# A two-layer mixture-of-experts trunk: routing taken off GpSimd, three experts in fixed places, the sorted lists made later, and the last weight tiles in the right pool

## The chip, the cores and the metric

The kernel runs on one core of a Trainium2 chip. The metric is the device time of one execution in microseconds (us). The core's engines are TensorE (PE in the profile; PEld is its weight load), VectorE (DVE), ScalarE (ACT), GpSimd (POOL) and SyncE (SP), which issues most of the transfers; SPq in a view is SyncE's queue.

## The reference, cut to what matters

1,024 tokens of 1,024 values go through two layers. A layer is a mixer (layer 0: gated DeltaNet and a diagonal state space; layer 1: dilated attention), an output projection with residual and layer norm, and a mixture of experts (MoE), again with residual and layer norm:

```python
x <- LayerNorm(alpha * x + sublayer(x)), alpha = (2*DEPTH)**0.25
D_MODEL = 1024; SEQ = 1024; EXPERT_FF = 512
MOE_GROUPS = 4; EXPERTS_PER_GROUP = 8; N_EXPERTS = 32; MOE_TOP_K = 2
```

Each token picks the best of four groups by its logits, then two of the group's eight experts; the sum of the two experts' outputs, silu(x Wg) * (x Wu) times Wd each, is weighted by gates made from the logits. How many tokens an expert gets is known only in the run.

## The kernel before, in words

**Stages.** By time of the trace: mixer of layer 0 and its output stage to about 650 us, MoE of layer 0 to 1201, its combine, the value projection and attention to 1880, the output stage of layer 1, its MoE from 1915 to 2458, the last combine to the end. The Tile framework orders the instructions of each engine by a timeline of its own; `issue_after(x)` lets an instruction be placed only after x.

**Output stage and routing.** `out_stage` works through eight token tiles of 128 rows. `logits` (`lgP`, `lgd`, `lg`) gives the router's logits, `route` picks experts and counts each token's place in its expert (`rM`, `rrk`, `rcnt`), `layer_norm` writes the normed rows to `hd` in memory (`hd<-or`). Of tile 7, the last, the norm's scale runs on ScalarE and its product with g and sum with b on GpSimd (L223, L226). At the end of `route` stand the token lists: `first` (lists of the large places; its first FIXED = 2 are experts 0 and 1 as they are), made at L354 and L355. `sort` (`osort`, `soP`, `soQ`) then ranks the 32 experts by their counts and writes `order`, `first` of places 2 to 15 and `small`; `gates` the gates and each token's `place`; `overflow` (`ofP`, `over`) plans blocks for experts with too many tokens. All three stand in the output stage.

**MoE.** 32 experts, six weight loads of 1 MB each (`wraw<-in_wm`, L458). Places 0 to 15 are large (128 tokens, `large`): each half tile of weights is split into a high part on ScalarE (`whi`, L486) and the remainder on VectorE (`wlo`, L489), and TensorE multiplies hi and lo parts of rows and weights three times (L528, L529, L546). Twelve halves a large expert. Places 16 to 31 are small (64 tokens, `small`), multiplied straight from the loaded tiles (L583, L599). The sequence is 0, 1, then per j the smalls s_j and s_(j+8) and two larges. A gather (L495, GpSimd) fetches an expert's rows of `hd` by its list; TensorE transposes them (`px`, L503), ScalarE and VectorE split them (`xh`, `xl`); one gather serves two smalls. Outputs are scattered to `yd` by GpSimd. After the fourth expert `table` writes sixteen index columns (`tab`, L428), read only in the overflow loop. Loads go in a ring of 17 tiles, ten in the left pool (`RAW`) and seven in the right (`RAWB`); two, later three, are in flight; the first ten are issued during the output stage. The halves have a ring of six. `moe_rest` holds the overflow loop, which runs zero times here, behind a barrier of all engines.

**Behind the MoE.** In layer 0 the value projection's four weight loads (`wraw<-in_wv`, L916) go into tiles of the left pool, in the ring's size, and two tiles of `hd` (`ca`) are loaded ahead. In layer 1 all eight are, in a pool that begins behind the place of the ring's last tiles, and `fg`, `fb` (norm weights, L191) after them. `combine` loads `yd` (`cy`), and in layer 1 TensorE sums gate-weighted rows (`cp`, L758); in four tiles (`SUMMED` = 1, 3, 5, 7) ALPHA * rows too, in the other four VectorE adds it (L762).

Of the kernel before, what the change touches and what calls it, by code (L numbers as in the profile page):

```python
# [32 lines left out]
FIXED = 2  # L33
# [120 lines left out]
class Trunk:  # L154

    SUMMED = (1, 3, 5, 7)

# [201 lines left out]
    def sort(self, R, first, small, order, ps):  # L359
# [3 lines left out]
        w = R["sort"]  # L363
        key, hot, tmp, tab = w[:NE, 0:32], w[:NE, 32:64], w[:NE, 64:96], w[:NE, 128:256]
        kp, rank = w[:NE, 96:97], w[:NE, 97:98]
        ident = self.ident[:NE, :NE]
        nc.vector.scalar_tensor_tensor(key, R["cnt"][:NE], float(NE), self.c("keyb")[:NE], op0=OP.mult, op1=OP.add)
# [6 lines left out]
        nc.tensor.transpose(p[:NE, :128], R["tab"], self.ident)  # L374
# [8 lines left out]
        nc.vector.tensor_copy(R["rank"], p[:, 96:128])  # L383
# [83 lines left out]
    def weights(self, src):  # L467
# [11 lines left out]
        for c in range(2):  # L479
# [126 lines left out]
    def moe(self, l, hd, yd, first, small, order, place, xp, wk, ps):  # L606
# [32 lines left out]
        next(run)  # L639
        next(run)  # L640
        for i in range(NE):
# [12 lines left out]
            if i == 3:  # L654
                with tc.issue_after(st.ins):
                    self.table(l, place)

# [24 lines left out]
    def overflow(self, R, over, ps):  # L682
# [3 lines left out]
        w = R["sort"][:BLOCKS]  # L686
        cap, c, cum, one, le, f = (w[:, i * NE:(i + 1) * NE] for i in range(6))
        ci = R["over"][:BLOCKS]

        idx = self.c("pidx")[:BLOCKS]  # L690
        nc.vector.tensor_scalar(cap, R["rank"][:BLOCKS], float(LARGE) - 0.5, None, op0=OP.is_lt)
        nc.vector.scalar_tensor_tensor(c, cap, -64.0, R["cnt"][:BLOCKS], op0=OP.mult, op1=OP.add)
# [24 lines left out]
    def ahead(self, l, hd, p, ts):  # L717
# [1376 lines left out]
```

## Time and profile before

| what | value |
|---|---|
| runs | 2517.41, 2521.05, 2521.86 us, median 2521.05 |
| the profiled execution's own time | 2522.76 us |
| its span | 2520.9 us |
| TensorE busy | 2276.8 us, 90% |
| VectorE busy | 1466.6 us, 58% |
| ScalarE busy | 1146.6 us, 45% |
| GpSimd busy | 485.0 us, 19% |
| MoE of layer 0, first transposes to the last matmul | 657.58 to 1201.1 us |
| MoE of layer 1, end of its last matmul | 2458.35 us |

Busy shares are averages over stages with different limits. A view of stretches tells, for each piece of the span, the busy time of each engine, the clock granted to TensorE (PEclk, a share of 2.4 GHz) and the mean busy share of the DMA engines. A row of waits names the waiting engine and line, whom it waited for, the total, how often and the longest. A row of a timeline begins with start and duration.

### The profile page before, as it was taken

How to read it: one execution, taken by the hardware profiler on the slowest of the kernel's cores; microseconds unless marked ns; L12 is line 12 of the kernel's file. 1: busy time of each engine (PE TensorE's matmuls, PEld its weight loads, DVE VectorE, ACT ScalarE, POOL GpSimd, SP SyncE). 2: the span in 40 equal slices, each digit the busy share in tenths (PEclk: the TensorE clock that was granted, in tenths of full speed). 3: DMA queues.
4: the chain of work that ended last, by engine and by line, in shares of the span. 5: the costliest groups of instructions: out<-in, count | busy, mean ns of one | idle time of the engine just before them, and what ended most of it. 6: DMA issues, size and time to landing. Idle time of an engine off the chain costs nothing. (4 is left out here: it accounts for less than half of the span.)

```text
span 2520.9 us, 33905 instructions
## 1 busy us (share of the span) xinstructions
PE 2276.8 (90%) x11950; PEld 1629.8 (65%) x11950; DVE 1466.6 (58%) x2901; ACT 1146.6 (45%) x1871; POOL 485.0 (19%) x566
## 2 busy tenths in 40 slices
PE   7999999899697999998599999997996979999986
PEld 5888888678454555555477777775784545555552
DVE  7655656556853555554554766766468535555545
ACT  5436353442453444443324666666325534444432
POOL 1445433102231111110001111103113311111100
PEclk9999999899798999999799999998997989999997
DMA  4222222272599999999531000102725999999986
GB/s 162 61 64 50 57 79 68 102 272 86 220 365 401 411 404 402 400 399 390 178 124 34 30 31 26 41 24 83 270 74 206 375 398 410 405 405 407 401 334 252
DMA packets 179198, 560.82 MB, mean 222 GB/s; under 512 B 59200, under 2 KB 96448, under 8 KB 129360
## 3 DMA queue, kind: packets, MB, share of 16 engines
q1 hardware_dynamic: 163920, 525.01, 55.1%
q0 software_dynamic: 15104, 33.60, 3.6%
q8 instruction: 96, 1.57, 0.2%
q14 instruction: 78, 0.64, 0.1%
HBM read 518.76 MB, written 55.36 MB: 228 GB/s over the span
## 5 line engine op out<-in xcount | busy, mean ns | idle before, releaser
L489 DVE TENSOR_TENSOR wlo<-wraw,whi 128x1024 fp32r<-128x1024 f32 x380 | 447.8, 1220 | 139.9 <-ACT whi L486 136.9
L486 ACT ACTIVATE whi<-wraw 128x1024 fp32r<-128x1024 f32 x384 | 384.4, 1053 | 76.2 <-PE pu L529 36.2
L583 PE MATMUL pgs<-wraw,xs 128*64 128x512 f32 x1024 | 241.3, 603 | 0.0
L583 PEld LDWEIGHTS pgs<-wraw,xs 128*64 128x64 f32 x1024 | 70.1, 138 | 133.4 <-issue 129.9
L172 PE MATMUL pj<-xTh,phi 128*128 128x512 f32 x320 | 131.9, 417 | 13.6 <-ACT xTh L449 13.6
L1072 POOL TENSOR_TENSOR plo<-praw,phi 128x256 fp32r<-128x256 f32 x64 | 50.2, 786 | 437.6 <-ACT phi L1071 291.4
L172 PE MATMUL pj<-xTh,plo 128*128 128x512 f32 x320 | 132.5, 415 | 0.0
L172 PE MATMUL pj<-xTl,phi 128*128 128x512 f32 x320 | 131.1, 410 | 0.0
L971 DVE CUSTOM_DVE_ANT_0 sm<-s,amask 128x1024 f32<-128x1024 f32 (+7 forms) x128 | 96.6, 756 | 51.5 <-PE s L967 49.6
L528 PE MATMUL pg<-whi,xh 128*128 128x512 f32 x256 | 107.0, 418 | 18.9 <-ACT whi L486 13.8
L599 PE MATMUL pos<-wraw,hs 128*64 128x512 f32 x512 | 118.6, 598 | 5.7 <-ACT xh L449 3.3
L988 PE MATMUL pp<-cf,sm 128*128 128x128 f32 x576 | 100.8, 285 | 22.8 <-ACT pt L992 18.0
L172 PE MATMUL opo<-ohi,oyp 128*128 128x512 f32 x392 | 115.7, 403 | 2.4 <-DVE oyp L450 2.4
L1088 PE MATMUL pj<-xTh,phi 128*128 128x512 f32 x256 | 114.6, 448 | 2.9 <-ACT phi L1071 1.0
L528 PE MATMUL pg<-wlo,xh 128*128 128x512 f32 x256 | 108.2, 423 | 8.1 <-DVE wlo L489 7.8
L551 POOL DMA_INDIRECT yd<-ot,first x32 | 38.0, 1188 | 369.2 <-issue 178.8
L975 ACT ACTIVATE sm<-sm,st 128x1024 f32<-128x1024 f32 (+7 forms) x128 | 99.1, 775 | 18.7 <-DVE st L974 16.4
L988 PEld LDWEIGHTS pp<-cf,sm 128*128 128x128 f32 x576 | 68.4, 143 | 57.8 <-ACT pt L992 50.0
L528 PE MATMUL pg<-whi,xl 128*128 128x512 f32 x256 | 103.4, 404 | 0.0
L529 PE MATMUL pu<-wlo,xh 128*128 128x512 f32 x256 | 102.4, 400 | 0.0
L529 PE MATMUL pu<-whi,xl 128*128 128x512 f32 x256 | 102.3, 400 | 0.0
L529 PE MATMUL pu<-whi,xh 128*128 128x512 f32 x256 | 102.2, 399 | 0.0
(543 smaller groups left out, 5195.7 us busy)
## 6 DMA issues: line engine op xcount, KB each, us to landing
wraw<-in_wm SPq DMA_DIRECT2D x384, 1024.0 KB, 8.3
cy<-yd SPq DMA_DIRECT2D x32, 512.0 KB, 7.3
praw<-in_win SPq DMA_DIRECT2D x40, 256.0 KB, 2.7
oraw<-in_wo SPq DMA_DIRECT2D x16, 512.0 KB, 3.3
hd<-or SPq DMA_DIRECT2D x16, 512.0 KB, 3.2
ca<-hd SPq DMA_DIRECT2D x16, 512.0 KB, 5.9
praw<-in_wqk SPq DMA_DIRECT2D x64, 128.0 KB, 2.3
oy<-ytd SPq DMA_DIRECT2D x14, 448.0 KB, 4.5
```

The costliest lines, as they stand in the source:

```text
L172: self.last = self.nc.tensor.matmul(*args, **kw).ins
L486: nc.scalar.activation(hi, r[:, h], AF.Copy)
L489: eng.tensor_tensor(lo, r[:, h], hi.bitcast(F32), op=OP.subtract)
L528: nc.tensor.matmul(pg, x[:, k], w[:, 0:512], start=s, stop=z)
L529: nc.tensor.matmul(pu, x[:, k], w[:, 512:1024], start=s, stop=z)
L583: nc.tensor.matmul(pg[r].rearrange("p (g f) -> p g f", g=2), x[:, k], w[:, k % 2, a], start=(k == 0), stop=(k == KT - 1))
L599: nc.tensor.matmul(po[r], hs[:, f % 2, f // 2], W[f // 2][:, o:o + 512], start=(f == 0), stop=(f == 3))
L971: nc.vector.tensor_tensor_reduce(out=sm[:, :n], in0=s[:, :n], in1=am[:, 1024 - n:1024], scale=1.0, scalar=-3e38, op0=OP.add, op1=OP.max, a ...
L975: nc.scalar.activation(sm[:, :n], sm[:, :n], AF.Exp, bias=st[:, 1:2], accum_out=st[:, 2:3])
L988: nc.tensor.transpose(pp[:, (j - j0) * 128:(j - j0 + 1) * 128], sm[:, j * 128:(j + 1) * 128], self.ident)
L1072: nc.gpsimd.tensor_tensor(lo, r, hi.bitcast(F32), op=OP.subtract)
L1088: nc.tensor.matmul(p, w[:, o], x[:, k, cs], start=(k == 0 and i == 0), stop=(k == KT - 1 and i == 2))
```

## The change

Seven things change. (1) The norm of tile 7 runs like that of tiles 0 to 6, but with its sum on VectorE; the first two `wlo` halves go to VectorE too. (2) FIXED is 3: experts 0, 1 and 2 come first and need no sorted list; then s0, s8, 3, 4 and so on. (3) `sort` is issued in the MoE, after the first `xl`, and `overflow` after `table`. (4) What they need is kept in a small tile `ov`. (5) The last five weight loads (187 to 191), which the ring would put in the left pool, go to the right pool, where they wait for the tiles of loads 180 to 184. (6) The value weights load into the tile that later holds V, in the left pool, and in layer 1 the rows of h have tiles of their own there; neither waits for ring tiles that the last loads would hold, and their pool's offset is gone. (7) The last combine: tiles 0 to 3 get ALPHA * rows in TensorE's sum, before `yd` is there; tiles 4 to 7 have it added by VectorE.

```diff
-FIXED = 2
+FIXED = 3
...
-    def layer_norm(self, r, mv, g, b, adder, spare=False):
+    def layer_norm(self, r, mv, g, b, adder):
...
-        if spare:
-            last = nc.scalar.activation(r, r, AF.Copy, scale=mv[:, 7:8])
-            nc.gpsimd.tensor_tensor(r, r, g, op=OP.mult)
-        else:
-            nc.vector.scalar_tensor_tensor(r, r, mv[:, 7:8], g, op0=OP.mult, op1=OP.mult)
+        nc.vector.scalar_tensor_tensor(r, r, mv[:, 7:8], g, op0=OP.mult, op1=OP.mult)
...
-        raw = self.raw_ring[self.at % len(self.raw_ring)]
+        n = len(self.raw_ring)
+
+        raw = self.raw_ring[self.at % n if self.at < NE * 6 // n * n else -1]
...
-            eng = nc.gpsimd if self.at == 1 else nc.vector
-            with after(eng):
-                eng.tensor_tensor(lo, r[:, h], hi.bitcast(F32), op=OP.subtract)
+            with after(nc.vector):
+                nc.vector.tensor_tensor(lo, r[:, h], hi.bitcast(F32), op=OP.subtract)
...
+        with tc.issue_after(self.hold["x"].ins):
+            self.sort(ov, first, small, order, wk, ps)
         next(run)
...
                 with tc.issue_after(st.ins):
                     self.table(l, place)
+                    self.overflow(ov, over, wk, ps)
...
+            for u in range(4):
+                P[u] = ps.tile([128, D], F32, name="cp", tag="cp", bufs=4)
+                for c in range(2):
+                    h = slice(c * 512, (c + 1) * 512)
+                    nc.tensor.matmul(P[u][:, h], al, rows[u][:, h], start=True, stop=False)
...
-                if t in self.SUMMED:
+                if t in P:
                     nc.scalar.activation(a, p, AF.Copy, accum_out=st[:, 0:1])
...
+            act, _ = self.layer_norm(r, mv, g, b, nc.vector if t == NT - 1 else nc.gpsimd)
+            nc.sync.dma_start(hd[ts, :], r)
             if t in BATCH:
                 self.route(BATCH[t], t + 1, R, lg, first, wk, ps)
-            act, add = self.layer_norm(r, mv, g, b, nc.gpsimd, t == NT - 1)
-            nc.sync.dma_start(hd[ts, :], r)
-        R["sort"] = wk.tile([128, KT * 128], F32, name="osort", tag="orT", bufs=1)
         with self.tc.issue_after(R["end"].ins):
-            self.sort(R, first, small, order, ps)
             self.gates(R, lg, gate, place, rp)
-            self.overflow(R, over, ps)
...
-            r = self.raw_ring[0].tile([128, 2048], F32, name="wraw", tag="wraw")
+            r = V[:, 2 * a:2 * a + 2]
             with self.tc.issue_after(self.flight[-1]):
-                self.nc.sync.dma_start(r, self.I["wv"][a])
-            R.append(r)
-        return R
...
-                        vp.tile([128, 8192 + (NE * 6 % (RAW + RAWB)) * 2048], F32, name="used")
-                    there = self.ahead(l, hd, vp, range(NT if l else 2))
+                    rows = [vp.tile([128, D], F32, name=f"ca{t}") for t in range(NT if l else 2)]
+                    g, b = (vp.tile([128, D], F32, name=n) for n in ("fg", "fb"))
+                    self.ahead(l, hd, rows)
```

VectorE at the start of the MoE of layer 0, before: from the fixed places of `first`, with the first two halves (L489) that VectorE has, to the first `xl`.

```order
L355 TENSOR_SCALAR first_5159<-first_5159 128x2
L367 SCALAR_TENSOR_TENSOR osort<-rcnt,cf_58 32x32
L404 TENSOR_TENSOR gsh<-lg,rmax 128x32
L408 TENSOR_TENSOR ge_6185<-rmax 128x8
L489 TENSOR_TENSOR wlo<-wraw,whi 128x1024
L368 TENSOR_TENSOR osort<-osort,cf_58 32x32
L489 TENSOR_TENSOR wlo<-wraw,whi 128x1024
...
L382 CAST order_5158<-soQ 1x32
...
L714 CAST over_5156<-ofP 1x48
L450 TENSOR_TENSOR xl<-px,xh 128x512
L489 TENSOR_TENSOR wlo<-wraw,whi 128x1024 x2
```

The same place of VectorE in after.

```order
L348 TENSOR_SCALAR first_5160<-first_5160 128x3
...
L483 TENSOR_TENSOR wlo<-wraw,whi 128x1024 x4
...
L443 TENSOR_TENSOR xl<-px,xh 128x512
L360 SCALAR_TENSOR_TENSOR osort<-ov_5157,cf_58 32x32
L483 TENSOR_TENSOR wlo<-wraw,whi 128x1024 x2
...
L483 TENSOR_TENSOR wlo<-wraw,whi 128x1024 x4
L375 CAST order_5159<-soQ 1x32
...
L443 TENSOR_TENSOR xl<-px,xh 128x512
L691 TENSOR_SCALAR ovw<-ovw 24x32
L483 TENSOR_TENSOR wlo<-wraw,whi 128x1024
```

Sort and overflow (`osort`, `ovw`) stood ahead of the first `xl`; now they stand behind it, singly among the halves, and four halves stand between `first` and `xl`.

GpSimd around the table, before (`first` after `<-hd` or `<-ot` is a large place, `small` a small one):

```order
L551 DMA yd<-ot,first_5159 2048x1024 x2
L495 DMA xg<-hd,first_5159 128x1024
L602 DMA yd<-ots,small_5157 4096x512 x2
L428 DMA tab<-tokv,place_5160 36864x1 x16
L495 DMA xg<-hd,small_5157 128x1024
```

GpSimd around the table in after.

```order
L545 DMA yd<-ot,first_5160 2048x1024 x2
L489 DMA xg<-hd,first_5160 128x1024
L596 DMA yd<-ots,small_5158 4096x512
L421 DMA tab<-tokv,place_5161 36864x1 x16
L489 DMA xg<-hd,small_5158 128x1024
L596 DMA yd<-ots,small_5158 4096x512
```

The table's sixteen writes stood behind both small experts' outputs; now they stand behind the first one's.

SyncE at the end of the MoE of layer 1, before:

```order
L458 DMA wraw<-in_wm 128x2048
L725 DMA ca_21097<-hd 128x1024
...
L725 DMA ca_21111<-hd 128x1024
L191 DMA fg<-in_lnfg 128x1024
L191 DMA fb<-in_lnfb 128x1024
L668 COMPARE_AND_BRANCH
```

SyncE at the same place in after.

```order
L453 DMA wraw<-in_wm 128x2048
L188 DMA fg<-in_lnfg 128x1024
L188 DMA fb<-in_lnfb 128x1024
...
L453 DMA wraw<-in_wm 128x2048
L720 DMA ca_21066<-hd 128x1024
...
L720 DMA ca_21073<-hd 128x1024
L665 COMPARE_AND_BRANCH
```

The loads of the norm weights stand seven weight loads earlier; the eight tiles of h stand right ahead of the barrier's branch.

## Rows read from the trace of the kernel before

**Rows 1.** Stretches, layer 0: busy PE, PEld, DVE, ACT, POOL; PEclk; DMA share; GB/s

```profile
640.00:660.00 20.00, 7.39 (x49) 5.22 (x49) 16.48 (x94) 1.34 (x4) 5.01 (x4) 0.50 0.26 95
660.00:700.00 40.00, 38.71 (x174) 27.68 (x172) 29.26 (x29) 24.09 (x27) 4.53 (x4) 0.97 0.93 353
760.00:780.00 20.00, 10.13 (x38) 4.45 (x38) 1.38 (x2) 1.19 (x2) 3.32 (x4) 0.62 1.01 400
780.00:860.00 80.00, 78.36 (x359) 46.06 (x360) 39.77 (x44) 34.31 (x44) 10.91 (x10) 1.00 1.01 412
```

**Rows 2.** TensorE's waits in layer 0's MoE: total, times, longest

```profile
PE px L503 <- DMA xg<-hd,small: 14.0, 1, 14.0
PE pg L528 <- ACT whi L486: 6.8, 4, 1.7
...
PE pg L528 <- DVE wlo L489: 4.1, 9, 0.5
```

**Rows 3.** Waits of SyncE's queue in the same stretch

```profile
SPq L458 <- DMA wraw<-in_wm: 402.0, 176, 4.7
```

**Rows 4.** Timeline of SyncE's queue at the end of layer 1's MoE

```profile
2426.08 9.59 SPq L458 DMA_DIRECT2D wraw<-in_wm  x4
2451.13 8.06 SPq L725 DMA_DIRECT2D ca<-hd  x8
...
2468.32 5.61 SPq L738 DMA_DIRECT2D cy<-yd  x10
```

**Rows 5.** Timeline of TensorE at the same place

```profile
2454.70 3.65 PE L599 MATMUL pos<-wraw,hs 128*64 128x512 f32 x16 [0.52 <-DVE hs L592]
2472.44 3.75 PE L758 MATMUL cp<-cy,cdg 128*128 128x512 f32 x4 [14.08 <-DMA cy<-yd]
```

**Rows 6.** TensorE's waits in layer 1's MoE

```profile
PE px L503 <- DMA xg<-hd,small: 13.3, 1, 13.3
```

**Rows 7.** Timeline of VectorE in layer 0's last routing

```profile
630.05 1.62 DVE L259 SCALAR_TENSOR_TENSOR lg<-lgd,ln_mv,orb 128x36 f32<-128x36 f32 x1
...
631.87 2.29 DVE L300 SCALAR_TENSOR_TENSOR rt<-rM,rt 128x96 f32<-128x96 f32 x1
634.09 4.72 DVE L317 TENSOR_TENSOR rt<-rM,cf 128x96 bf16<-128x96 f32 x2
638.73 0.21 DVE L286 SCALAR_TENSOR_TENSOR rt<-lg,rmax,cf 128x4 f32<-128x4 f32 x1
...
640.52 0.42 DVE L317 TENSOR_TENSOR rt<-rM,cf 128x96 bf16<-128x96 f32 x2
...
646.98 0.17 DVE L355 TENSOR_SCALAR first<-first 128x2 int32<-128x2 int32 x1
```

**Rows 8.** Timeline of GpSimd in layer 0, from the last routing to the table

```profile
629.26 2.35 POOL L223 TENSOR_TENSOR or<-or,og 128x1024 f32<-128x1024 f32 x1 [5.50 <-ACT or L222]
...
647.43 3.44 POOL L495 DMA_INDIRECT xg<-hd,first  x1 [1.06 <-DVE ge L408]
659.83 1.00 POOL L495 DMA_INDIRECT xg<-hd,first  x1 [8.96 <-PE px L503]
...
760.53 1.05 POOL L495 DMA_INDIRECT xg<-hd,small  x1 [0.30 <-issue]
```

**Rows 9.** Groups of instructions of one form in 657:700: count, busy, mean ns

```profile
L489 DVE TENSOR_TENSOR wlo<-wraw,whi 128x1024 fp32r<-128x1024 f32 x20 | 24.4, 1224 | 3.0 <-ACT whi L486 2.2
...
L450 DVE TENSOR_TENSOR xl<-px,xh 128x512 fp32r<-128x512 f32 x4 | 2.7, 685 | 1.5 <-ACT xh L449 1.5
```

**Rows 10.** DMA issues in 645:660: count, KB each, us to landing

```profile
xg<-hd,first POOLq DMA_INDIRECT x2, 6.5
```

**Rows 11.** Timeline of TensorE where layer 0's experts begin

```profile
657.42 0.23 PE L712 MATMUL ofP<-cf,osort 24*1 24x24 f32 x2 [1.30 <-DVE osort L709]
657.58 1.97 PE L503 MATMUL px<-cf,xg 128*128 128x128 f32 x8
...
692.60 7.08 PE L583 MATMUL pgs<-wraw,xs 128*64 128x512 f32 x30
```

More of the change, by code (lines that the diff above doesn't have):

```diff
@@ L604, in small, with moe @@
             in_=ot, in_offset=None, bounds_check=4 * S - 1, oob_is_err=False)
-    def moe(self, l, hd, yd, first, small, order, place, xp, wk, ps):
+    def moe(self, l, hd, yd, first, small, order, place, ov, over, xp, wk, ps):
         nc, tc = self.nc, self.tc
@@ L680, in moe_rest, with overflow @@
                 pass
-    def overflow(self, R, over, ps):
+    def overflow(self, ov, over, wk, ps):
         nc = self.nc
-        w = R["sort"][:BLOCKS]
-        cap, c, cum, one, le, f = (w[:, i * NE:(i + 1) * NE] for i in range(6))
-        ci = R["over"][:BLOCKS]
+        w = wk.tile([NE, 256], F32, name="ovw", tag="ovw", bufs=1)[:BLOCKS]
+        cap, c, cum, one, le, f, ci = (w[:, i * NE:(i + 1) * NE] for i in range(7))
+        ci = ci.bitcast(I32)
+        cnt, rank = ov[:BLOCKS, 0], ov[:BLOCKS, 1]
         idx = self.c("pidx")[:BLOCKS]
-        nc.vector.tensor_scalar(cap, R["rank"][:BLOCKS], float(LARGE) - 0.5, None, op0=OP.is_lt)
-        nc.vector.scalar_tensor_tensor(c, cap, -64.0, R["cnt"][:BLOCKS], op0=OP.mult, op1=OP.add)
+        nc.vector.tensor_scalar(cap, rank, float(LARGE) - 0.5, None, op0=OP.is_lt)
+        nc.vector.scalar_tensor_tensor(c, cap, -64.0, cnt, op0=OP.mult, op1=OP.add)
         nc.vector.tensor_scalar(c, c, 63.0, 0.0, op0=OP.add, op1=OP.max)
@@ L715, in overflow, with ahead @@
         nc.vector.tensor_copy(over[:, 2, 0:1], cum[0:1, NE - 1:NE])
[L717 removed]
+    def ahead(self, l, hd, rows):
         nc = self.nc
[L720 to L721 removed]
         with self.tc.issue_after(self.flight[-1]):
[L723 to L725 removed]
+            for t, r in enumerate(rows):
+                nc.sync.dma_start(r, hd[t * 128:(t + 1) * 128, :])
                 if l == 0:
[L727 to L728 removed]
+                    nc.scalar.activation(r, r, AF.Copy, scale=ALPHA)
     def combine(self, l, hd, yd, gate, g, b, rows, wk, ps, done):
@@ L814, in out_products, with out_stage @@
                     yield MM, 0
-    def out_stage(self, l, ytd, W, last, po, first_ps, xd, hd, gate, first, small, order, place, over, rp, wk, wp,
+    def out_stage(self, l, ytd, W, last, po, first_ps, xd, hd, gate, first, place, ov, rp, wk, wp,
                   part):
@@ L1982, in run @@
                 with self.pool(f"ow{l}", 2) as wk, self.pool(f"owp{l}") as wp:
-                    self.out_stage(l, ytd, *out, xd, hd, gate, first, small, order, place, over, pools[2], wk, wp,
+                    self.out_stage(l, ytd, *out, xd, hd, gate, first, place, ov, pools[2], wk, wp,
                                    pools[0])
@@ L1992, in run @@
                     self.part_ring = [pools[0]] * 4 + [partb] * 2
-                    xg = self.moe(l, hd, yd, first, small, order, place, xp, wk, ps)
+                    xg = self.moe(l, hd, yd, first, small, order, place, ov, over, xp, wk, ps)
                     for q in reversed(pools):
@@ L2024, in run @@
                     nc.scalar.activation(wk.tile([128, 1], F32, name="warm", bufs=1), self.ident[:, 0:1], AF.Sqrt)
-                    self.combine(l, hd, yd, gate, *there, wk, ps, done)
+                    self.combine(l, hd, yd, gate, g, b, rows, wk, ps, done)
                 vp.release()
```

72 lines of the change are left out of this document (28 added, 44 removed).

## The prediction

> **What bounds the kernel now.** I read first the table of stretches around the start of layer 0's MoE [rows 1]. In 780:860 TensorE is busy 78.36 of 80 us at a granted clock of 1.00, while the DMA engines are full too (1.01). Which of the two sets the pace is told by TensorE's waits in that MoE [rows 2]: they name gathered rows, ScalarE's high halves and VectorE's low halves, and no weight load has a row. SyncE's queue, in turn, waits 402.0 us for loads in flight [rows 3], and at the end of layer 1 the last loads are issued by 2426.08 + 9.59 = 2435.7 [rows 4] while the last matmuls that read them begin at 2454.70 [rows 5], 19.0 us later. So the MoE is bound by TensorE, with the transfers a little ahead of it; a load that starts earlier is worth nothing by itself, and each microsecond at which TensorE stands still or crawls counts in full. Three such places are touched. TensorE is slow until the first expert begins (640:660: 7.39 of 20 us busy, clock 0.50). It is held once for 14.0 us by a gather for the small experts [rows 2], in layer 1 for 13.3 us [rows 6]. And between the last expert and the first sum of the last combine lie 2472.44 - (2454.70 + 3.65) = 14.1 us [rows 5].
>
> **The start of a MoE.** The chain is: VectorE's routing of the last token tile, `first`, GpSimd's gather, the transposes px, the first expert. On VectorE, three short operations are long while GpSimd works beside them: 630.05 takes 1.62 us, 631.87 takes 2.29 and 634.09 takes 4.72 for two, and the next begins at 638.73; the same L317 takes 0.42 for two at 640.52, when GpSimd is idle [rows 7]. GpSimd's work there is the scale, the add and two low halves from 629.26 on [rows 8]. The change takes all four off GpSimd. What remains of 630.05 to 638.73 (8.7 us): about five short operations of 0.2 to 0.4 (1.3 us) and, if the scheduler puts them in between, VectorE's own product and add of the last tile. I price these two at one low half each (1.22 us [rows 9]), 2.4 together; 8.7 - 3.7 = 5.0 us. `first` is then ready at 646.98 - 5.0 = 642.0.
> The gather issues at 647.43 and a gather there lands 6.5 us after its issue (median of the two, [rows 10]), at 653.9. But px starts only at 657.58, right after the overflow plan's matmul at 657.42 [rows 11], which stands in front of it on TensorE. The change moves that matmul, with sort and overflow, behind the first expert. The new gather issues near 642.4 and would land near 648.9. Against it: that first gather took 3.44 us on GpSimd beside two low halves, the next one 1.00 [rows 8], and now four low halves stand in a row on VectorE (the second fence on VectorE). With 0 to 2.5 us more for that, px comes at 648.9 to 651.4: 6.2 to 8.7 us earlier. Bounds: 3 (the gather waits for all four halves, 4 x 1.22 = 4.9, and less of the stretched time returns) and 10. **I take -7 us for each layer**; layer 1 repeats the pattern of layer 0.
> The Trainium skill, page "SBUF — State Buffer", section "Who interferes with whom", says that a VectorE instruction with two SBUF inputs contends with a GpSimd instruction that reads SBUF, and not with one that only writes there. The three stretched rows agree; the 3.44 us of the gather, which is not such an operation, beside low halves with two SBUF inputs, does not. By that rule the gather would take 1.00 as at 659.83 and px would come about 2.4 to 4.9 us earlier still; that is the last rival below.
>
> **The wait for the small experts' rows.** In before the sixteen table writes stand on GpSimd between the fourth expert's output and the next small gather, which issues only at 760.53 [rows 8]; TensorE waits 14.0 us for it and then runs at a mean clock of 0.62 in 760:780 [rows 1]. In after the same sixteen stand in the order after the scatter of s0, but the sequence now is 0, 1, 2, s0, s8, 3, 4, and then the next gather for smalls: behind s0, TensorE has s8 and two large experts (17.5 us each, below) to do. The fence of GpSimd shows that the gather of expert 3 is ahead of the table, and that of expert 4 is not far behind. **-14.0 becomes about 3 left: -11** in each layer, bounds -14 (all gone) and -5 (a gather for expert 4 waits in its turn).
>
> **The front of three large experts.** This is what the change pays. Two large experts and their start take TensorE 692.60 - 657.58 = 35.0 us [rows 11], 17.5 each; three take 52.5. VectorE's work beside them is: 36 low halves, of which four stand before px: 32 x 1.224 = 39.2 us; six operations on xl at 0.685 (4.1) [rows 9]; hdn, hl and ot of three experts, nine operations of a like size (6.2); the remaining sort and overflow operations, about 40 at the 0.2 us of their like (the short rows [rows 7]), 8. Sum 57.5 us, more than TensorE's 52.5. In before the sort and the plan came ahead of px, and two larges instead of three were followed by two smalls, which need nothing of VectorE's halves. If VectorE never stood still, TensorE would be 57.5 - 52.5 = 5 us late. But it does not reach that: in 660:700 it is busy 29.26 of 40 us, 73%, since it waits for ScalarE's halves and for free buffers. At 73% the front would take 57.5 / 0.73 = 78.8, 26 us late. The order adds that the casts of `order` stand on VectorE behind four low halves (the second fence), and that until they are done the PSUM bank which the next expert's transposes use is held by sort's result. **I take +15**, between the ends and nearer the middle, as the ring of six halves lets VectorE run somewhat ahead; bounds +3 and +20 (over that is a rival). Sum of each layer: -7 - 11 + 15 = **-3 us**.
>
> **The ends.** The last five loads now wait for five slots of the right pool, read as late as the last large expert's down tiles. The 19.0 us between the last issue and the last reader [rows 4, 5] hide it down to a slack of some microseconds; price 0, and if the cover is gone up to +5 in each layer. In layer 0 the value weights and two tiles of h were issued ahead already; nothing is taken off the path: 0, bounds 0 and +3. In layer 1, eight tiles of h waited in SyncE's queue until 2451.13 for buffers, and the two row loads and the barrier came behind them, so that the first yd load is issued at 2468.32 [rows 4]. The order now has the row loads seven weight loads earlier and h behind the last load. The barrier needs the last expert's output (2454.70 + 3.65 = 2458.35, then its scatter), so only part returns. The first four tiles' ALPHA sums move into the 14.1 us gap; in exchange VectorE adds four tiles in a row at the end. I take **-3**, bounds -7 and 0.
>
> **Sum.** Twice -3 and -3 is -9 us. The profiled execution took 2522.76 us against a median of 2521.05, 1.7 above it; on the scale of the median 2521 - 9 = **2512 us**.
>
> **Rivals.** (B) The front takes back all that both gains give: +18 in each layer instead of +15, and the last row -3 to 0. Then 2518 to 2524. For it speaks VectorE's sum, which is above TensorE's even at full share. (C) VectorE keeps up, as after 700, where TensorE waits hardly for it: front +3, -15 each layer, 2521 - 33 = 2488. Against it: the sum above. (D) Slower: the front loses more than 18 us in each layer, the point from which this decides. The mechanism is the clock: TensorE pauses at each late half, and after a pause the clock granted is lower (0.62 in 760:780 after the 14.0 us, 0.50 in 640:660, where the engine idles between short pieces [rows 1]), so that matmuls within the front take up to twice their time. With +23 in each layer and an end of 0 it gives 2521 + 10 = 2531, 2536 with the right pool's loads late besides. (E) The page's rule holds for the gather: front as forecast, start -11 instead of -7, 2521 - 17 = 2504. (F) That the change does not do what it says: the order shows that it does, except that a table write could still stand ahead of a needed gather; this lies in the bound -5.
>
> **How the numbers follow.** Forecast 0.34 (2512, its own range 2504 to 2519), B 0.28, C 0.09, D 0.23, E 0.06. Within 0.2% (2516 to 2526, about what a measurement of this kernel can tell from no change): 0.05 of the forecast, 0.20 of B and 0.01 of D, 0.26. Faster: 0.29 + 0.03 + 0.09 + 0.06 = 0.47; slower: 0.05 + 0.22 = 0.27. The range leaves out most of C and the far part of D: 2492 to 2538.
>
> **What would show it.** Right: px of the first expert near 650 from a start like before's, the wait for small rows at 3 us or less, waits for wlo and whi of some 15 us within the first three experts, and no wait for a wraw load. Wrong: waits of TensorE for VectorE over 20 us with a granted clock under 0.9 in that stretch (D); under 5 us of them (C); a wait on wraw in the last 20 us of a MoE (the right pool); a gather of about 1 us beside the four low halves (E). What would make the sum wrong most easily is the share VectorE reaches in the front: each tenth of it is worth about 7 us in each layer.

## The result, and the profile after

The changed kernel takes 2493.88 us (median of 4 runs, 2492.90 to 2498.11) against 2519.23 (4 runs, 2511.86 to 2521.86): ratio 0.9907, 95% interval [0.9883, 0.9932]. The forecast was 2512, faster. The sign held. The time lies in the whole range (2492 to 2538), 1.9 us above its lower end, and outside the range of the forecast itself (2504 to 2519); the gain of 25 us is 2.8 times the 9 that were forecast.

The gain is best read stage by stage. The table gives, for each layer, the time from the last logits (`lgd`) to the first transposes (`px`); the front, to the end of s8's output matmuls; the block up to the end of s9, which holds the table's writes; the five later blocks of two smalls and two larges, each to the end of the next second small, summed; and what follows to the last expert's end. The end is from there to the end of the span. All are differences of rows of TensorE's and VectorE's timelines, one profile each. Of TensorE's tiles, `pg` and `pu` are a large expert's two products for the hidden rows, `ph` the transposed hidden rows and `po` the product with the down weights; `pgs`, `phs` and `pos` are those of a small expert.

| kernel | layer | logits to px | front | table block | five later | last | sum | end |
|---|---|---|---|---|---|---|---|---|
| before | 0 | 27.9 | 73.0 | 78.6 | 328.7 | 63.2 | 571.4 | |
| before | 1 | 27.6 | 72.3 | 77.8 | 327.7 | 61.9 | 567.3 | 62.5 |
| changed | 0 | 18.8 | 93.5 | 72.5 | 332.7 | 42.9 | 560.4 | |
| changed | 1 | 16.6 | 92.3 | 72.8 | 342.8 | 43.0 | 567.5 | 58.0 |

One large expert moves from the last piece to the front, so these two go together: +20.5 and -20.3 in layer 0, +20.0 and -18.9 in layer 1. Of the 24.7 us by which the span is shorter, 11.0 come from layer 0's MoE, none from layer 1's (0.2 longer: what its start and its table block give is eaten by the five later blocks, +15.1), 4.5 from the end, 3.0 from the way between layer 0's last expert and attention, and 6.4 from the mixer and attention, which the change does not touch. So 15.3 us stand in the stages that the forecast had summed, against its 9; the other 9.4 it had at nothing, and no run here shows that the change brings them.

VectorE's timeline at the start of layer 0's MoE, after (start, duration). It answers [rows 7].

```profile
629.04 1.28 DVE L218 SCALAR_TENSOR_TENSOR or<-or,ln_mv,og 128x1024 f32<-128x1024 f32 x1
...
630.58 1.22 DVE L219 TENSOR_TENSOR or<-or,ob 128x1024 f32<-128x1024 f32 x1
...
631.95 0.41 DVE L310 TENSOR_TENSOR rt<-rM,cf 128x96 bf16<-128x96 f32 x2
...
640.55 0.17 DVE L348 TENSOR_SCALAR first<-first 128x3 int32<-128x3 int32 x1
...
641.14 4.62 DVE L483 TENSOR_TENSOR wlo<-wraw,whi 128x1024 fp32r<-128x1024 f32 x4
```

GpSimd's timeline after, for [rows 8].

```profile
641.95 1.49 POOL L489 DMA_INDIRECT xg<-hd,first  x1 [2.01 <-DVE gef L411]
649.64 1.00 POOL L489 DMA_INDIRECT xg<-hd,first  x1 [6.20 <-PE px L497]
...
739.08 1.09 POOL L421 DMA_INDIRECT tab<-tokv,place  x1 [0.30 <-issue]
...
760.81 1.50 POOL L489 DMA_INDIRECT xg<-hd,small  x1 [0.30 <-issue]
```

TensorE where the experts begin, after, for [rows 11].

```profile
647.39 1.97 PE L497 MATMUL px<-cf,xg 128*128 128x128 f32 x8 [7.07 <-DMA xg<-hd,first]
```

The product (1.28) and the sum (1.22) of the last tile stand on VectorE, L310 is short again (0.41 for two, 4.72 before), and `first` is ready 11.9 us behind the last logits instead of 17.3. The first gather takes 1.49 us while VectorE works on four low halves, and px starts 5.4 us after its issue.

TensorE's waits after, in layer 0's MoE (total, times, longest), for [rows 2].

```profile
PE pg L522 <- ACT whi L481: 12.6, 8, 2.0
PE px L497 <- DMA xg<-hd,first: 7.9, 2, 7.1
PE pg L522 <- DVE wlo L483: 6.4, 12, 0.9
...
PE px L497 <- DMA xg<-hd,small: 1.9, 2, 1.4
...
PE po L540 <- ACT whi L481: 1.6, 1, 1.6
```

The same in layer 1's, for [rows 6].

```profile
PE pg L522 <- ACT whi L481: 11.2, 7, 1.7
PE po L540 <- ACT whi L481: 9.8, 6, 1.6
...
PE px L497 <- DMA xg<-hd,small: 2.1, 1, 2.1
```

The one wait for small rows of 14.0 and 13.3 us is 1.9 and 2.1 now. New is the row of po: in layer 1 the down matmuls wait six times 1.6 us for a high half. Here is one of the six, on TensorE's timeline:

```profile
2149.98 1.94 PE L577 MATMUL pgs<-wraw,xs 128*64 128x512 f32 x8
2151.85 0.66 PE L529 MATMUL ph<-cf,hdn 128*128 128x128 f32 x4
2154.14 0.73 PE L540 MATMUL po<-whi,hh 128*128 128x512 f32 x2 [1.63 <-ACT whi L481]
2155.40 1.22 PE L540 MATMUL po<-wlo,hh 128*128 128x512 f32 x2 [0.52 <-DVE wlo L483]
2156.41 1.05 PE L540 MATMUL po<-whi,hl 128*128 128x512 f32 x2
2157.27 1.05 PE L540 MATMUL po<-whi,hh 128*128 128x512 f32 x2
...
2158.75 0.63 PE L540 MATMUL po<-whi,hl 128*128 128x512 f32 x2
```

The transposes `ph` are followed by nothing that could run while ScalarE and VectorE split the hidden rows and the down tile; TensorE waits 1.63 and 0.52 us, and the pairs of matmuls behind that take 1.05 to 1.22 us instead of the last row's 0.63. ScalarE makes the high halves of the down tile only behind the hidden rows (`hh`):

```profile
2152.54 0.60 ACT L442 ACTIVATE hh<-ph 128x512 fp32r<-128x512 f32 x1 [2.08 <-PE ph L529]
2153.04 3.89 ACT L481 ACTIVATE whi<-wraw 128x1024 fp32r<-128x1024 f32 x4
```

Bare transposes alone are not it. The kernel before has them in layer 1 too:

```profile
2098.30 0.66 PE L535 MATMUL ph<-cf,hdn 128*128 128x128 f32 x4
2099.64 0.73 PE L546 MATMUL po<-whi,hh 128*128 128x512 f32 x2 [0.69 <-ACT hh L449]
```

But there ScalarE has made two high halves (from 2096.79 on) ahead of `hh` (2098.99), and TensorE waits 0.69 us (its next pairs take 0.63). Where the halves stand behind `hh` in the kernel before, eight matmuls of `pgs` follow the transposes. In layer 1 of the changed kernel both come together in every one of the five later blocks.

SyncE's queue at the end of layer 1, after, for [rows 4].

```profile
2412.05 11.84 SPq L453 DMA_DIRECT2D wraw<-in_wm  x5
2423.93 7.61 SPq L720 DMA_DIRECT2D ca<-hd  x8
2443.68 14.68 SPq L748 DMA_DIRECT2D cy<-yd  x16
```

The first yd load is issued 5.5 us behind the last expert's end (2438.2), where it was 10.0 us behind it [rows 4, 5].

### The profile page after: what moved, and what is told of

It reads as the page before. It is cut to its first block, busy times and chain, and to the rows that moved or that the text cites. A ratio compares the mean times of both kernels' runs of the same rounds, so it can differ in the third digit from the quotient of the medians.

```text
span 2496.2 us, 33852 instructions
## 1 busy us (share of the span) xinstructions
PE 2277.7 (91%) x11950; PEld 1628.5 (65%) x11950; DVE 1454.3 (58%) x2909; ACT 1144.1 (46%) x1869; POOL 463.2 (19%) x558
## 5 line engine op out<-in xcount | busy, mean ns | idle before, releaser
L169 PE MATMUL pj<-xTh,phi 128*128 128x512 f32 x320 | 131.6, 416 | 13.1 <-ACT xTh L442 13.1
L975 PE MATMUL pp<-cf,sm 128*128 128x128 f32 x576 | 100.3, 284 | 20.3 <-ACT pt L979 15.0
```

What stands on the lines that cost most here:

```text
L169: self.last = self.nc.tensor.matmul(*args, **kw).ins
L975: nc.tensor.transpose(pp[:, (j - j0) * 128:(j - j0 + 1) * 128], sm[:, j * 128:(j + 1) * 128], self.ident)
```

## The experiments

Ratios are against the kernel before, with their 95% intervals. The table at the end of this section has the stages of all twelve.

**The pin on the order (a_pin).**

```diff
-            nc.tensor.transpose(ph[:, f * 128:(f + 1) * 128], hdn[:, f * 128:(f + 1) * 128], self.ident)
+            self.turned = nc.tensor.transpose(ph[:, f * 128:(f + 1) * 128], hdn[:, f * 128:(f + 1) * 128], self.ident)
...
-            for a, r in enumerate(sides):
+            with self.tc.issue_after(self.turned.ins) if k else nullcontext():
+                for a, r in enumerate(sides):
```

> The changed kernel, with one pin more: of a small expert that follows a large one, the gate matmuls from the second k-tile on are placed behind the transposes of that large expert's hidden rows. Theory O (order): in layer 1 of the changed kernel the scheduler put those matmuls ahead of the transposes in six of the blocks of two smalls and two larges, so that the down matmuls follow the transposes bare; each time TensorE waits 1.6 us for a high half and 0.5 us for a low half and then runs some matmuls at half clock. With the pin a block of layer 1 takes 65 to 66 us instead of 67.8 to 69.5, layer 1's MoE is 12 to 16 us shorter, layer 0's 0 to 4, and the time is 2476 to 2483 us against 2494. Rival T (transfers): layer 1's blocks are longer because the weight loads set the pace there (18 of them stand in a row in the chain that ended last); then the pin changes nothing, 2491 to 2497.

Measured: 2491.66 us, 0.9882 [0.9864, 0.9900]. TensorE's waits in four later blocks of layer 1, 2059.6 to 2323.2:

```profile
PE pg L522 <- ACT whi L481: 5.1, 3, 1.7
...
PE ph L529 <- DVE hdn L526: 3.7, 4, 1.2
```

These four take 263.9 us, 274.3 in the changed kernel. The waits of po are gone; a smaller one, of the transposes for the hidden rows, has come (3.7). So in these blocks theory O holds against T: the transfers let them be 2.6 us shorter each. The time does not show it: 2491.66 lies in T's range and far from O's, and layer 1's MoE is 6.9 us shorter, not 12 to 16. The pin also changes the order in the table block, 78.7 and 79.1 us, against 72.5 to 77.5 in the profiles of the changed kernel's order (last table), which gives part of the gain back.

**The old pools (a_oldpools, a_l1pools).** The first undoes the last five loads' place, the value weights' and the rows'; the second, whose edit this is, undoes the loads' and the rows' place in layer 1 alone.

```diff
-        raw = self.raw_ring[self.at % n if self.at < NE * 6 // n * n else -1]
+        raw = self.raw_ring[self.at % n if self.at < NE * 6 // n * n or self.layer else -1]
...
                         vp = alloc("cr")
+                        vp.tile([128, 8192 + (NE * 6 % (RAW + RAWB)) * 2048], F32, name="used")
```

> The changed kernel with the last five loads, the value weights and the rows of h placed as in the kernel before (ring order, value weights in the right pool's tiles and split behind the barrier, rows of h behind the offset). The order of TensorE in both MoE stages is that of the changed kernel. Theory P: the new pools gain 3 us between the MoE of layer 0 and attention and 2 to 4 at the end, and the 15 to 22 us by which the last five loads start later are hidden (the last matmuls still begin 5 us after their weights land): 2499 to 2502 us, MoE ends where they were within 1 us. Rival R (right pool): the late loads hold up the end of each MoE; then both MoE end 3 to 5 us earlier than in the changed kernel, and the time is 2487 to 2494.

> The changed kernel with the ring order of the last five loads and the offset of the rows of h as before in layer 1 alone; layer 0 stays as changed. Theory P: 2496 to 2498 us (rows of h and the first sums of the last combine come later), MoE of layer 1 as long as in the changed kernel. Rival R: the MoE of layer 1 ends 3 to 5 us earlier, and what the late rows cost is less, so 2490 to 2493.

Measured: 2511.93 us, 0.9960 [0.9947, 0.9974], and 2506.05 us, 0.9936 [0.9920, 0.9953]. R falls: layer 1's MoE takes 550.9 and 551.3 us from px on, 550.9 in the changed kernel, though in the changed kernel the first of the last five loads is issued only at 2412.05 (SyncE's row above), 22 us behind the load before it, and in the other two 2 to 3 us behind it. P has the sign, but its price for layer 1 was 2 to 4 and is 12. In a_l1pools SyncE's queue at the end of layer 1 reads:

```profile
2397.64 41.80 SPq L720 DMA_DIRECT2D ca<-hd  x8
2439.48 0.44 SPq L188 DMA_DIRECT2D fg<-in_lnfg  x1
2439.96 1.01 SPq L188 DMA_DIRECT2D fb<-in_lnfb  x1
2451.97 14.93 SPq L748 DMA_DIRECT2D cy<-yd  x16
```

and the longest wait there:

```profile
DVE al L734 <- DMA fb<-in_lnfb: 19.7, 1, 19.7
```

The eight rows of h hold the queue for 41.8 us, since their places are those of ring tiles still in use; the norm weights come behind them at 2439.5, and the barrier that every engine waits at holds until fb has landed. The end takes 68.3 us, 58.0 with the new pools. Over all kernels it takes 59.6 to 69.6 us with the old pools (five kernels) and 56.9 to 58.0 with the new ones (nine). For the further 6 us of a_oldpools the profile names no place in layer 0 (560.9 against 560.4 us, and 167.2 against 166.5 to attention); its runs lie between 2502.78 and 2516.75, the profiled one at the low end. That part is open.

**Early lists (a_early).** `sort` and `overflow` are called before the first expert.

```diff
+        with tc.issue_after(self.hold[nc.vector].ins):
+            self.sort(ov, first, small, order, wk, ps)
+            self.overflow(ov, over, wk, ps)
         run = enter(seq[0])
...
-        with tc.issue_after(self.hold["x"].ins):
-            self.sort(ov, first, small, order, wk, ps)
...
-                    self.overflow(ov, over, wk, ps)
```

> The changed kernel with the sort and the overflow plan placed ahead of the first expert, as in the kernel before, three fixed experts kept. Theory L: late lists are what lets the first transposes start at once; with the plan's matmul in front of them again the first expert begins 6 to 9 us later in each layer, and the front of three large experts is no faster without those operations on VectorE (it is not what bounds it): 2506 to 2512 us. Rival V (VectorE bounds the front, as predicted): the front gets 8 us or more faster in each layer without the 40 small operations between the halves, which pays for the later start: 2490 to 2498.

Measured: 2503.63 us, 0.9939 [0.9922, 0.9955]; its runs go from 2494.24 (the profiled one) to 2508.56. The time is 2.4 us under L's range and above V's. px comes 5.7 and 6.6 us later, about as L has it, and the front is 2.8 and 2.7 us longer, not shorter, so V falls. The profile's sum of stages, though, is about that of the changed kernel (560.4 and 565.1), since other blocks are shorter. The medians give late lists 10 us, this profile none; what they are worth stays between the two.

**The pin from the third block on, the spread table, and both (a_pin2, a_spread, a_both).**

```diff
+            with self.tc.issue_after(self.turned.ins) if k and self.at > 60 else nullcontext():
...
-                    self.table(l, place)
+            if 3 <= i < 19:
+                with tc.issue_after(st.ins):
+                    self.table(l, place, i - 3, tabs)
```

> The changed kernel with the pin of the first run, but only from the third block of two smalls and two larges on; the order of TensorE before that is that of the changed kernel. Theory O (order): the front and the block with the table's writes take what they take in the changed kernel (92 to 94 us and 72 to 73), the later blocks of layer 1 65 to 67 us, so that layer 1's MoE is 11 to 14 us shorter than 550.9 and the time is 2481 to 2486 us. Rival D (transfers): behind the front a block can't be shorter than 24 loads take; then the later blocks of layer 1 stay at 67 to 69 us, and the time at 2489 to 2494.

> The changed kernel with the table's sixteen writes spread over sixteen experts, one behind each output from the fourth expert on, in place of sixteen in a row. Theory G (GpSimd's queue): the block that holds the table takes 72.5 us in the changed kernel, 7 more than its neighbours, since gathers and outputs queue behind 22.5 us of writes; spread, it takes 65 to 67, and the time is 10 to 14 us lower, 2480 to 2484. Rival F: the excess of that block is that of the order of TensorE and the first gather for smalls, not of the table; then it stays at 70 to 73, 2490 to 2495.

> Pin from the third block on and spread table together. If both theories (O and G) hold and each gain is TensorE's own, they add up: 2468 to 2475 us. If the transfers set a floor right behind, less than half of the sum remains: 2480 to 2486.

Measured: 2490.11 us, 0.9872 [0.9846, 0.9898]; 2482.70, 0.9837 [0.9817, 0.9857]; 2469.63, 0.9792 [0.9774, 0.9809]. The pin alone gives less than O said: the later blocks of layer 1 take 66.6 to 68.2 us each (338.4 in all, 342.8 without), though the waits of po are gone, and blocks and time lie about where rival D has them. D's reason is not borne out: the same 24 loads a block pass in 63.9 to 66.8 us in layer 1 of the kernel before, and in the changed kernel's later blocks of layer 1 each load is issued 31 us or more ahead of its first reader. So the waits of po are a real cost, 1 to 3 us a block, but not all that parts this order from the one before (327.7); most of the rest is waits of other names, as the next section shows. The table is settled: spread, its block takes 68.6 and 66.0 us, near G's 65 to 67 and below F's 70 to 73, and the time is G's. GpSimd there:

```profile
733.07 1.38 POOL L592 DMA_INDIRECT yd<-ots,small  x1 [5.42 <-ACT ots L591]
734.76 1.09 POOL L417 DMA_INDIRECT tab<-tokv,place  x1 [0.31 <-issue]
743.03 1.05 POOL L485 DMA_INDIRECT xg<-hd,small  x1 [7.18 <-PE px L493]
...
746.28 0.97 POOL L417 DMA_INDIRECT tab<-tokv,place  x1 [0.30 <-issue]
```

One write stands behind an output, and the small gather is issued at 743.03, 8.3 us behind the first write; in the changed kernel it waits for sixteen, 21.7 us (739.08 to 760.81 above). Both together beat their sum, and no floor shows up to there; this is the fastest of the versions that compute everything.

**Parts alone, on the kernel before (b_route, b_fixed3, b_pools).** The norm of the last tile and the first halves on VectorE (part 1 of the change); FIXED = 3 (the constant of part 2); the new pools (parts 5 and 6, whose edit stands under "The change"). Of the first edit one place is shown.

```diff
-            act, add = self.layer_norm(r, mv, g, b, nc.gpsimd, t == NT - 1)
+            act, _ = self.layer_norm(r, mv, g, b, nc.vector if t == NT - 1 else nc.gpsimd)
```

```diff
-FIXED = 2
+FIXED = 3
```

> The kernel before with one part of the change alone: the last tile's norm and the first two low halves on VectorE in place of GpSimd. Theory: the list of the first experts is 5 to 6 us earlier in each layer, and the first transposes too (the plan's matmul in front of them moves with it), 22 to 23 us behind the last logits instead of 27.9; the rest of the MoE as before, so 2509 to 2512 us against 2520.6. Rival (transfers): the weight loads behind the first ten start earlier by as much; if they don't, or if the MoE is bound by them, the gain is lost by the end of each MoE: 2517 to 2521.

> The kernel before with three fixed experts as the only edit; lists, norm and pools stay as they were. Theory: the wait for the small experts' first rows behind the table, 14.0 us, falls to 3 or less, the block that holds the table goes from 78 to 71 to 74 us, and the front gets longer by the 20 us of one large expert that the last block loses. Each layer gains 4 to 7 us if the order of the later blocks stays as good: 2507 to 2513. Rival O: the scheduler's order of the later blocks moves too, and they take 67 to 69 us in place of 65 to 66; then the gain is gone, 2518 to 2526.

> The kernel before with the new pools alone (last five loads in the right pool, value weights in the tile of V and split ahead of the barrier, rows of h and the norm weights' loads without ring tiles to wait for). The way from the last expert to the end of the kernel takes 62.5 us in the kernel before and 58.0 in the changed one; with the changed combine on the old pools it took 68. Theory B (the barrier of layer 1 waits for the norm weights, which stand in SyncE's queue behind the rows of h): the pools alone give 8 to 10 us there, 53 to 55, and the time is 2509 to 2513. Rival C: the changed combine carries the gain, and the pools alone give 0 to 4: 2516 to 2521.

Measured: 2528.01 us, 1.0025 [1.0015, 1.0035]; 2527.97, 1.0032 [1.0018, 1.0046]; 2517.45, 0.9983 [0.9970, 0.9997]. The first two lose what they gain, and are slower than either of their ranges says. b_route has `first` 5.3 us earlier, but px only 2.7 and 3.7. Its first gather takes 5.63 us while VectorE makes four halves (GpSimd's row, then VectorE's),

```profile
639.22 5.63 POOL L490 DMA_INDIRECT xg<-hd,first  x1 [1.66 <-issue]
...
638.95 2.34 DVE L484 TENSOR_TENSOR wlo<-wraw,whi 128x1024 fp32r<-128x1024 f32 x2
641.42 2.34 DVE L484 TENSOR_TENSOR wlo<-wraw,whi 128x1024 fp32r<-128x1024 f32 x2
```

and sort's steps wait behind these halves, so that the plan's matmul, right ahead of px (651.44), comes at 651.27. Its table block is 9.5 and 8.0 us shorter, but its five later blocks take 339.8 and 337.4 us, 11 and 10 more than before. Its rows of h are issued at 2448.55, as the last expert ends, and its end takes 69.6 us, 7.1 more. In b_fixed3 the wait for the small rows falls from 14.0 to 6.6 us, the table block to 70.8 and 71.2, and the five later blocks rise to 344.1 and 338.3, 68.8 and 67.7 each: rival O. Its waits in layer 0:

```profile
PE po L546 <- ACT whi L486: 8.2, 5, 1.6
PE px L503 <- DMA xg<-hd,small: 6.6, 2, 5.9
```

The row of po, which the kernel before does not have, is there again. b_pools leaves both MoE about as they were (543.9 and 542.1 us from px on, 543.5 and 539.7 before) and shortens the end from 62.5 to 57.3; that lies between B and C, and the time, 4 us lower, in C's range.

**No low halves in the front (a_nolo).**

```diff
+            if self.at <= 18:
+                W.append((hi, hi))
+                continue
             lo = part.tile([128, 1024], F32R, name="wlo", tag="wlo")
```

> The changed kernel without the low halves of the first 18 loads (three large experts): TensorE multiplies the high half in their place, so it does the same work, and VectorE is rid of 36 operations of 1.2 us there (part of the computation is left out, the first three experts are wrong by that). Theory V (the prediction's: VectorE bounds the front): the front of three larges and two smalls, 93.5 and 92.3 us in the changed kernel, falls by 10 us or more, to 78 to 83. Theory N (TensorE bounds it, VectorE keeps up): it falls by 3 us at most, to 89 to 93. The order of the later experts differs from that of the changed kernel, so only the front is compared.

Measured: 2469.21 us, 0.9797 [0.9771, 0.9824]; the front takes 88.5 and 88.7 us instead of 93.5 and 92.3. Neither bound holds: with VectorE's halves the front takes 5.0 and 3.6 us more, no more than that. TensorE's order in the front differs too, so these are rough prices. (The kernel leaves out the low parts of the first three experts' weights, so its time is no gain. It is 25 us lower than the changed kernel's, much of it by later blocks in another order: 320.5 us in layer 0, 332.7 in the changed kernel.)

**The old combine (both_comb)**, on a_both: ALPHA times the rows right ahead of the gate-weighted rows, in every other tile.

```diff
-            for u in range(4):
+            for u in ():
...
+                if t % 2:
+                    for c in range(2):
+                        h = slice(c * 512, (c + 1) * 512)
+                        nc.tensor.matmul(p[:, h], al, a[:, h], start=True, stop=False)
```

> The changed kernel with pin and spread table, but the last combine as in the kernel before (ALPHA times the rows summed by TensorE in every other tile, right ahead of the gate-weighted rows). With the pin and the spread table the end takes 57.3 us, of which 9.3 are the first four tiles' ALPHA sums, which begin only behind the barrier. Theory B: the pools carry the gain of the end; with the combine of before the end takes 53 to 57 us, and the time is 2465 to 2470. Rival C: the changed combine is needed; the end takes 60 to 63 us, and the time is 2472 to 2476.

Measured: 2471.83 us, 0.9804 [0.9781, 0.9827], end 56.9 us against 57.3. By the end's length B holds; the time is 1.8 us above B's range and just under C's, and 2.2 above a_both, within the spread of its own runs (2468.09 to 2474.97). The changed combine is worth nothing that can be told; the pools carry the end.

| kernel | logits to px | front | table block | five later | last | sum | end |
|---|---|---|---|---|---|---|---|
| a_pin | 18.1 / 16.8 | 91.8 / 92.0 | 78.7 / 79.1 | 332.0 / 331.3 | 40.1 / 41.6 | 560.7 / 560.8 | 57.7 |
| a_oldpools | 18.1 / 16.6 | 92.8 / 92.4 | 74.1 / 74.4 | 333.0 / 339.8 | 42.9 / 44.3 | 560.9 / 567.5 | 67.9 |
| a_l1pools | 18.0 / 16.6 | 92.7 / 92.8 | 77.5 / 74.6 | 332.6 / 341.0 | 42.9 / 42.9 | 563.7 / 567.9 | 68.3 |
| a_early | 24.5 / 23.2 | 96.3 / 95.0 | 71.9 / 69.6 | 330.4 / 336.8 | 37.3 / 40.5 | 560.4 / 565.1 | 57.3 |
| a_pin2 | 18.6 / 17.4 | 92.8 / 92.1 | 77.4 / 73.9 | 332.9 / 338.4 | 40.1 / 40.1 | 561.8 / 561.9 | 57.1 |
| a_spread | 18.1 / 16.7 | 92.9 / 92.5 | 68.6 / 66.0 | 328.8 / 341.3 | 42.9 / 44.3 | 551.3 / 560.8 | 57.9 |
| a_both | 18.1 / 16.8 | 92.5 / 92.0 | 68.4 / 67.1 | 329.1 / 334.6 | 40.1 / 40.1 | 548.2 / 550.6 | 57.3 |
| b_route | 25.2 / 23.9 | 77.4 / 75.0 | 69.1 / 69.8 | 339.8 / 337.4 | 58.0 / 58.0 | 569.5 / 564.1 | 69.6 |
| b_fixed3 | 27.8 / 27.1 | 92.0 / 92.6 | 70.8 / 71.2 | 344.1 / 338.3 | 42.8 / 42.9 | 577.5 / 572.1 | 59.6 |
| b_pools | 27.8 / 27.1 | 72.8 / 73.4 | 79.0 / 79.4 | 330.3 / 327.5 | 61.8 / 61.8 | 571.7 / 569.2 | 57.3 |
| a_nolo | 17.5 / 16.5 | 88.5 / 88.7 | 74.4 / 73.1 | 320.5 / 338.5 | 40.6 / 37.4 | 541.5 / 554.2 | 58.0 |
| both_comb | 18.2 / 16.6 | 92.4 / 92.2 | 68.2 / 65.7 | 328.7 / 337.7 | 40.1 / 41.7 | 547.6 / 553.9 | 56.9 |

(Layer 0 / layer 1.) The table block of the changed order goes from 72.5 to 77.5 us in profiles that share it (changed, a_oldpools, a_l1pools, a_pin2), so a difference of 5 us in that column means nothing between them; layer 0's sum goes from 560.4 to 563.7 in the first three of these, which share TensorE's whole order.

## Why the forecast was right in sign and wrong in size

**What bounds.** Right: no wait of TensorE names a weight load in either kernel, and most loads in the changed one are issued 25 to 40 us ahead of their first reader (the last five 12 to 15). Earlier loads gave nothing by themselves: in layer 1 load 184 is issued at 2379.7 instead of 2416.1, 36 us earlier, and the last expert ends 20 us earlier, as much as this MoE also starts earlier.

**The start, -7: measured -9.1 and -11.0.** The first half of the step was exact: `first` 5.3 us earlier against 5.0, product and sum at 1.28 and 1.22 against 1.22 each. The second half failed where it priced the gather by the row of 3.44 us and put up to 2.5 us on top: with the new order it takes 1.49 and 1.79 us, and px starts 5.4 and 4.9 us after its issue against the 6.5 to 9.0 that the step allowed. How the gather and the halves meet can be read from their ends. Here the first of the four halves ends 1.22 us behind 641.14, the gather ends at 641.95 + 1.49 = 643.44, 1.08 later. In b_route the fourth half ends at 643.76 and the gather at 644.85, 1.09 later. In the kernel before the second half ends at 649.78 (648.57 and 1.21) and the gather at 650.87, 1.09 later. In every kernel with halves there, in both layers, the gather ends 0.96 to 1.10 us behind the end of one of them, and a_nolo's gathers, without halves, take 1.21 and 1.09. So by its ends the gather is not slow but held: until a half ends, and then it takes its own 1 us. In the changed order it gets through behind the first half, in the kernel before behind the second and in b_route behind the fourth; what lets it through no run here shows. The Trainium skill, page "SBUF — State Buffer", section "Who interferes with whom", has VectorE's two-input operations contend with GpSimd instructions that read SBUF, not with those that only write there. These ends agree with it only if the gather counts as one that reads, which the prediction denied and no run here tests. Rival E's sign, a gather of about 1 us beside the halves, came near, but not as E has it, since by these ends the gather is held by them.

**The wait for the small rows, -11: measured -6.1 and -5.0.** The wait itself fell as said, 14.0 to 1.9 us. What failed is to take the wait for the price: the block kept 6.0 and 4.2 us over the mean of the later ones, in pieces under other names, since the other gathers and outputs of that block still queue behind sixteen writes. a_spread shows it: without that queue the block takes 68.6 and 66.0 us, where its later blocks take 65.8 and 68.3 on average.

**The front, +15: measured +0.2 and +1.1**, the term that was furthest off. The prediction's own sign for this term, some 15 us of waits for low and high halves within the first three experts, came out at 0.9 us in layer 0 and at none in layer 1, which was its sign for rival C. TensorE's one such wait from px to the end of the front:

```profile
PE pg L522 <- DVE wlo L483: 0.9, 1, 0.9
```

The sum of VectorE's work (57.5 us) may stand; what failed is the share that it reaches. It was set from 73% in a stretch in which VectorE did not have to hurry. In the front after it is busy 29.25 of 33.0 us, 89% (third figure of the row: PE, PEld, DVE, ACT, POOL):

```profile
647.40:680.40 33.00, 32.07 (x145) 25.54 (x146) 29.25 (x58) 22.87 (x26) 1.99 (x2) 0.91 0.48 182
```

An engine's share where it waits for others says what it was asked for, not what it can do. a_nolo puts VectorE's part at 4 to 5 us, and the step compared with 17.5 us for a large expert, while the one that leaves the last piece takes 20.3 and 18.9 there: moving it costs what it saves. Rival C was nearest to this term, and the time is nearest to C's 2488; but C gave 30 us to the two MoE, which together gave 10.8, so C as a whole is not borne out. Among the rivals' sums, B's upper end of 2524 has no term: +18 and an end of -3 to 0 give 2518 to 2521.

**The ends, 0 and -3.** The cover of the last five loads held: load 190 is issued at 2421.8, its reader begins at 2434.51, and the MoE is no longer for it (a_l1pools). Layer 1's end gave 4.5 us between these profiles; with the changed kernel's other parts in place the pools are worth 10 by the end's length (68.3 against 58.0) and 12 by the medians. The way from the last expert to attention's first product with V is 3.0 us shorter, but it is in a_oldpools too (167.2 us against 169.5 in before and 166.5 in the changed kernel), and with the new pools it goes up to 170.4 (a_spread), so nothing speaks for the value weights as the cause; it is open. From that product to the last of its kind attention takes 404.7 to 410.1 us over the fourteen profiles, though no kernel differs there; before's is the longest, the changed kernel's 405.0, and this puts 5.1 us into the difference of the two spans.

**What the sum did not have: the order of the blocks that the change does not touch,** +4.0 and +15.1. The scheduler places each engine's work by a timeline of its own; an edit at the start of a MoE shifts it and settles the later blocks in another pattern. In the changed kernel TensorE's order there is another one than before in both layers. Five blocks took 320.5 to 344.1 us over the runs with the same work in them, and TensorE's waits tell most of it. Summed over these blocks they are 16.8 and 16.2 us in the kernel before (layers 0 and 1), 19.4 and 28.4 in the changed one, 23.4 in layer 1 of a_pin2 and 20.4 in that of a_pin; over the fourteen kernels they go from 13.1 (layer 0 of a_nolo, 320.5) to 28.7 (layer 0 of b_fixed3, 344.1). Times of 308 us plus 1.2 for each us of wait meet all 28 stretches within 3.3 us, so what the order costs is TensorE's waits, nearly all for what ScalarE and VectorE make of rows and weights, and a little more than the waits themselves. Of layer 1's +15.1, 12.2 are waits. Layer 0's +4.0 is less sure: a_spread has the changed kernel's order of TensorE in these blocks and takes 328.8. b_fixed3 lost its gains there, b_route those of its table block, and in the changed kernel layer 1 lost all of them. The order of the changed kernel is fixed before it runs, and the bare transposes with the high halves behind them stand in it; the prediction went by the places of the edits alone.

So errors of both signs stood in the sum: in each layer the front was priced 14 to 15 us too high, the start gave 2 and 4 us more and the table block 5 and 6 less than said, and the later blocks, which the sum did not have, cost 4 and 15. That the stages of the sum gave 15.3 us in the forecast's direction is luck in part: in layer 1's MoE the errors cancel to nothing, and layer 0's gain stands only because its later blocks lost 4 us and not 15.

## What to carry to other kernels

Where a scheduler places the work, cost an edit on the order that comes out, over the whole loop and not at the edit alone; then pin the few places that matter, and check TensorE's waits over the whole loop. A wait that falls by 12 us may give back 6: ask what else stands in the queue that caused it, and spread such work (here sixteen writes, 6 to 9 us a layer). Loads that only a late stage needs should not stand in a queue behind loads that wait for buffers, when a barrier waits for all of them.

## What the hardware showed that was not expected

The same first gather, of the same size, took 1.09 to 1.83 us on GpSimd in the changed kernel and its variants, 3.34 to 3.44 in the kernel before and 5.60 to 5.63 in b_route, each time alike in both layers, and wherever VectorE's low halves ran beside it, it ended 0.96 to 1.10 us behind the end of one of them. And behind TensorE's waits of 1.63 and 0.52 us at 2154, its matmuls took up to twice their time, with a granted clock of 0.62 in that stretch, a mean of its two levels (1.2 and 2.4 GHz), and of 1.00, the higher one, in the stretch before the wait (the last three figures of a row are PEclk, DMA share and GB/s):

```profile
2146.00:2152.00 6.00, 6.00 (x26) 2.34 (x25) 0.92 (x2) 0.60 (x1) 0.00 (x0) 1.00 1.01 417
2154.00:2158.50 4.50, 3.84 (x9) 2.78 (x10) 4.38 (x4) 2.92 (x4) 0.00 (x0) 0.62 1.03 406
```
